# New costs for the clock that places the side chains of a hybrid decoder layer: non-urgent operations counted a third longer, and each change of engine charged

## The chip, the cores and the metric

The kernel runs on one core of one Trainium2 chip. The metric is the device time of one execution, in microseconds (us); lower is better. The same program is run several times and the median counts.

## The reference

One decoder layer over 512 tokens of width 2048, in float32:

```python
h = rms_norm(x, attn_norm_g)
proj = h @ w_in
ya = diff_attention(...)          # 4 heads, ALiBi, causal
yb = sliding_window_attention(...)  # 8 query heads, window 128, sinks
yc = rwkv7_time_mix(token_shift(rw, mu), ...)   # 16 heads of 64
x = x + concat(ya, yb, yc) @ w_out
h = rms_norm(x, ffn_norm_g)
gate, up = split(h @ w_gate_up)
x = x + (silu(gate) * up) @ w_down
return rms_norm(x, final_norm_g)
```

The RWKV part is a recurrence over time, `S = S * w + (S a) b + v k`, read out by `r`. The kernel does it in chunks of 64 steps, which needs the inverse of a triangular matrix per chunk.

## The kernel before, in words

Every large product is a stream of matrix multiplications over 128x512 tiles. A weight is split into a rounded half and a rest, as is the input, and three products of the halves are added. So one 128-column projection is 16 x 3 = 48 matmuls (`dense`, `dense_k`, L214 to L222). `sequence` (L347) runs a list of such items: one projection of the shared lora inputs, 24 for the eight RWKV pairs of heads (k, r and v of each pair), 12 for the four heads of differential attention, 6 for the sliding window, then two times 16 for the output projection (`wout_items`, L1031, 24 matmuls each) and the feed-forward part.

Everything else is cut into short steps, written as Python generators that stand in eight lanes: `rates` (decay and learning rate of a pair), `prep` (keys, transposes `bt`, products `gr`, `vt`, `bon`), `inverse` and `join` (the triangular inverse), `chain` (the recurrence over eight chunks: `z`, `u`, `S`, `y`), `post` (its normalisation `var` and gate `g`), the attention heads (`sa`, `wt`, `oa`, `sb`, `wtb`, `ob`) and `mixes`, which brings the mixers' outputs in for the output projection. After each matmul of a projection `pump` (L162) runs, while the kernel is being written, and asks of each lane whether its next step is due. It measures this with a clock of its own. `now` adds up the matmuls written so far. `free` holds, for VectorE (DVE) and ScalarE (ACT), until when their written work will keep them. `last` follows the step that is being written: when its last operation will be done. A step that yields no time of its own comes due `slack` (0.3) after `last`. So a longer `last` puts more projection matmuls between a step and the next one of its lane.

The program is static. The scheduler beneath keeps TensorE's (PE's) instructions in the written order and moves those of the other engines by its own estimate. Each engine then works its list from the top, and waits where an operand is not there.

Four places matter below.

- `prep` (L493): after `kn` (L506) come three ACT operations and eight DVE rows that end in `bk` (L526, L531). The next step transposes `bk` on PE (`bt`, L540). Ahead of it stands `while hp >= 2 and f"loop{hp - 2}" not in self.done: yield`. The tile `ar`, written first of the DVE rows after `kk` (L518), has two buffers, and the recurrence of the pair two before reads the older one until its last `y` matmul.
- `prep`, products `gr`: two rounds of 16 matmuls into the two buffers of the PSUM pool `pm`. Six masking operations on DVE (L574) empty a round. The next round, `vt`, `bon`, and the next pair's `z` and `pa` (L470, L475) use the same two buffers.
- `inverse` (L613) takes 30 small pairs of DVE operations (`xt`, `x`, L629 and L630). Then `x` is copied transposed by ACT (L633), both are written to DRAM and read back (L636, L637, L649, L651), and `join` multiplies (`pt`, then `po`, L658 and L668).
- `need` (L180): a projection's result can't be put away until an earlier pair's step is done. If it isn't, `need` moves `now` forward and writes due steps, with no projection matmuls between them. Below this is a drain.

Of the kernel before, what the change touches and what calls it, by code (L numbers as in the profile page):

```python
# [88 lines left out]
class Kernel:  # L89
    def __init__(self, tc, ins, out, dbg=None, stop=None):  # L90
        self.tc = tc
        self.nc = tc.nc
        self.i = ins
        self.out = out
        self.dbg = dbg or {}
        self.stop = stop
        self.lanes = [[], [], [], [], [], [], [], []]
        self.order = [self.lanes[j] for j in (2, 7, 6, 5, 0, 1, 3, 4)]
        self.done = set()
        self.flags = set()  # L100
        self.now = 0.0
        self.due = {}
        self.free = {"DVE": 0.0, "Activation": 0.0}
        self.last = 0.0
        self.slack = 0.3

    def col(self, name, j=0, n=P):
# [29 lines left out]
    def charge(self, ins):  # L137
        eng = str(ins.engine).split(".")[-1]
        if eng not in self.free or not ins.outs or not hasattr(ins.outs[0], "ap"):
            return  # L140
        n = math.prod(c for _, c in list(ins.outs[0].ap)[1:])
        if eng == "DVE":
            us = 0.14 + n * (0.0019 if ins.opcode == "StreamTranspose" or "Scan" in ins.opcode else 0.00104)
        else:
            us = 0.19 + n * 0.00085
        self.free[eng] = max(self.free[eng], self.now + 0.2) + us
        self.last = max(self.free[eng], self.last + us + 0.05)

    @contextlib.contextmanager
    def urgent(self):  # L150

        free = dict(self.free)
        for eng in free:
            self.free[eng] = min(free[eng], self.last + 0.3)
        with self.tc.high_priority():
            yield
        for eng in free:
            self.free[eng] = max(self.free[eng], free[eng] + 0.3)

# [1117 lines left out]
```

## Time and profile before

| | us |
|---|---|
| median of 3 runs (2480.7 to 2483.81) | 2481.95 |
| the profiled execution | 2481.82 |
| its span, first to last instruction | 2480.0 |
| PE busy in the span | 2419.3 |
| DVE busy | 1230.6 |
| ACT busy | 824.2 |
| mean granted PE clock | 0.988 |

A row of a timeline gives start, duration, engine, line, operation, output and inputs, shape and count; in brackets stands how long the engine had been idle before and what ended that. A row of a group gives busy time and the mean in ns, then the idle time before its instructions. A row of a stretch gives its ends and length, then the busy time of PE, of PE's weight loads, of DVE, ACT and POOL (GpSimd), the granted PE clock (1.00 is full speed) and the DMA share. `xcount` of an fp32 matmul counts its passes.

### The profile page before, as it was taken

The page shows a single profiled execution, that of the slowest core. Times are in us where ns is not written, and L with a number is a line of the kernel's source. Part 1 is how long each engine was busy: PE and PEld are TensorE (multiplying, and loading weights), DVE is VectorE, ACT ScalarE, POOL GpSimd, SP SyncE. Part 2 cuts the span into 40 slices and gives each one's busy share as a digit, 9 for nine tenths or more (in the row PEclk, how much of TensorE's full clock was granted, in tenths as well). Part 3 has the DMA queues.
Part 4 walks back from the last instruction along what each step waited for, and adds up shares of the span by engine and source line. Part 5 has one row for each costly group of instructions (what it writes and reads, how often), then busy time and mean ns, then how long its engine had stood idle before and what let it go on. Part 6 is the DMA issues. An engine that isn't in the chain of part 4 may idle for free.

```text
span 2480.0 us, 30228 instructions
## 1 busy us (share of the span) xinstructions
PE 2419.3 (98%) x12072; PEld 1921.0 (77%) x12072; DVE 1230.6 (50%) x2113; ACT 824.2 (33%) x1383; POOL 93.0 (4%) x117
## 2 busy tenths in 40 slices
PE   8999999989999999999999999999999999999997
PEld 6776666667677778888888888888888888888887
DVE  7587777776454544434343434343434334343437
ACT  5454555544443433322222222222222222222224
POOL 3000000000000002100000000000000000000006
PEclk9999999999999999999999999999999999999999
DMA  5222221213222423322322223232232322322224
GB/s 175 88 80 72 69 81 49 79 60 96 84 83 79 162 94 128 99 96 95 101 94 101 95 95 101 94 99 97 94 101 94 99 97 94 101 94 99 97 94 136
DMA packets 99054, 238.43 MB, mean 96 GB/s; under 512 B 30426, under 2 KB 39266, under 8 KB 98914
## 3 DMA queue, kind: packets, MB, share of 16 engines
q1 hardware_dynamic: 94018, 229.81, 28.7%
q10 hardware_dynamic: 4896, 6.69, 0.8%
q8 instruction: 95, 1.56, 0.2%
q14 instruction: 45, 0.37, 0.0%
HBM read 224.93 MB, written 11.53 MB: 95 GB/s over the span
## 4 chain that ended last, share of the span: by engine, by line
PE 91%; DVE 6%; ACT 1%; issue 1%; DMA 1%; POOL 0%; SPq 0%; DVEq 0%; ACTq 0%; POOLq 0%
PE pg L130 19%; PE pu L130 19%; PE pd L130 19%; PE po L130 7%; PE pd_k L130 4%; PE pd_r L130 3%; PE pd_v L130 2%; PE pd_va L130 2%; PE pd_qb L130 2%; PE pd_qa L130 2%; PE pd_ka L130 1%; PE z L130 1%; PE pd_l L130 1%; PE y L130 1%; PE gr L130 1%
## 5 line engine op out<-in xcount | busy, mean ns | idle before, releaser
L130 PE MATMUL pd<-al,wh_wd 128*128 128x512 f32 (+1 forms) x768 | 285.3, 371 | 0.5 <-DVE al L1127 0.5
L130 PE MATMUL pd<-ah,wh_wd 128*128 128x512 f32 (+1 forms) x768 | 285.5, 372 | 0.4 <-DVE y L1146 0.4
L130 PE MATMUL pd<-ah,wl_wd 128*128 128x512 f32 (+1 forms) x768 | 285.2, 371 | 0.0
L130 PE MATMUL pu<-x1h,wh_wu 128*128 128x512 f32 x704 | 274.3, 390 | 0.0
L130 PE MATMUL pu<-x1h,wl_wu 128*128 128x512 f32 x704 | 273.9, 389 | 0.0
L130 PE MATMUL pu<-x1l,wh_wu 128*128 128x512 f32 x704 | 273.9, 389 | 0.0
L130 PE MATMUL pg<-x1h,wh_wg 128*128 128x512 f32 x704 | 273.9, 389 | 0.0
L130 PE MATMUL pg<-x1h,wl_wg 128*128 128x512 f32 x704 | 273.9, 389 | 0.0
L130 PE MATMUL pg<-x1l,wh_wg 128*128 128x512 f32 x704 | 273.9, 389 | 0.0
L1146 DVE TENSOR_TENSOR y<-y,pd 128x512 f32<-128x512 f32 (+1 forms) x192 | 122.7, 642 | 207.7 <-PE pd L130 207.6
L207 ACT CAST wh_wd<-raw_wd 128x1024 fp32r<-128x1024 f32 x96 | 100.9, 1052 | 356.9 <-PE pd L130 177.2
L207 ACT CAST wh_wu<-raw_wu 128x1024 fp32r<-128x1024 f32 x88 | 92.7, 1053 | 366.7 <-PE pu L130 144.5
L207 ACT CAST wh_wg<-raw_wg 128x1024 fp32r<-128x1024 f32 x88 | 92.7, 1054 | 362.8 <-PE pg L130 144.9
L208 DVE TENSOR_TENSOR wl_wg<-raw_wg,wh_wg 128x1024 fp32r<-128x1024 f32 x88 | 107.8, 1225 | 171.4 <-ACT wh_wg L207 171.4
L208 DVE TENSOR_TENSOR wl_wu<-raw_wu,wh_wu 128x1024 fp32r<-128x1024 f32 x88 | 107.8, 1225 | 133.4 <-ACT wh_wu L207 133.4
L130 PEld LDWEIGHTS pd<-al,wh_wd 128*128 128x128 f32 x768 | 144.7, 188 | 25.7 <-DVE al L1127 0.8
L130 PEld LDWEIGHTS pd<-ah,wh_wd 128*128 128x128 f32 x768 | 144.7, 188 | 25.5 <-issue 0.5
L130 PEld LDWEIGHTS pd<-ah,wl_wd 128*128 128x128 f32 x768 | 144.7, 188 | 25.0
L130 PEld LDWEIGHTS pu<-x1h,wh_wu 128*128 128x128 f32 x704 | 132.2, 188 | 27.6 <-issue 0.2
L130 PEld LDWEIGHTS pu<-x1l,wh_wu 128*128 128x128 f32 x704 | 132.2, 188 | 27.6 <-issue 0.2
L130 PEld LDWEIGHTS pg<-x1l,wh_wg 128*128 128x128 f32 x704 | 132.2, 188 | 27.4
L130 PEld LDWEIGHTS pg<-x1h,wh_wg 128*128 128x128 f32 x704 | 132.2, 188 | 27.4
(340 smaller groups left out, 4155.1 us busy)
## 6 DMA issues: line engine op xcount, KB each, us to landing
raw_wd<-in_w_down SPq DMA_DIRECT2D x96, 512.0 KB, 3.2
raw_wg<-in_w_gate SPq DMA_DIRECT2D x88, 512.0 KB, 3.7
raw_wu<-in_w_up SPq DMA_DIRECT2D x88, 512.0 KB, 3.7
raw_wo<-in_w_out SPq DMA_DIRECT2D x32, 512.0 KB, 3.3
raw_k<-in_w_in SPq DMA_DIRECT2D x16, 512.0 KB, 3.7
raw_r<-in_w_in SPq DMA_DIRECT2D x16, 512.0 KB, 3.9
raw_v<-in_w_in SPq DMA_DIRECT2D x16, 512.0 KB, 3.8
x<-in_xT SPq DMA_DIRECT2D x16, 256.0 KB, 4.6
```

Source lines behind the costliest of these rows:

```text
L130: self.tc.keep_in_program_order(self.nc.tensor.matmul(out, lhsT, rhs, start=start, stop=stop))
L207: nc.scalar.copy(out=hi[:, :kn * m], in_=s)
L208: nc.vector.tensor_tensor(out=lo[:, :kn * m], in0=s, in1=hi[:, :kn * m].bitcast(F32), op=ALU.subtract)
L1146: nc.vector.tensor_tensor(out=o, in0=o, in1=ps, op=ALU.add)
```

## The change

Two fields are added. `charge`, which is called for each DVE and ACT instruction as it is written, multiplies the operation's cost by `share` (1.3, but 1.0 within `urgent`) where it extends `last`. It adds 0.15 where the engine differs from that of the operation charged before, and nothing where it is the same; it was 0.05 for each. `free` is counted as it was. `urgent` is used around the copies and updates of the recurrence (L691, L705, L713).

```diff
+        self.share = 1.3
+        self.on = None
...
         self.free[eng] = max(self.free[eng], self.now + 0.2) + us
-        self.last = max(self.free[eng], self.last + us + 0.05)
+
+        self.last = max(self.free[eng], self.last + us * self.share + (0.0 if eng == self.on else 0.15))
+        self.on = eng
...
+        share, self.share = self.share, 1.0
         with self.tc.high_priority():
             yield
+        self.share = share
```

No instruction's work changes; steps move. Lines of the changed kernel are 2, 4 or 6 higher than before. In PE's list 40 projection matmuls stand between `kn` and the first `bt` of pair 0 before and 51 now; of pair 1, 40 before and 49 now. From pair 2 on `bt` follows the recurrence of the pair two before. PE's rows from that recurrence's last `u` to `bt` of pair 3, before (r4 is the projection running there):

```order
L130 MATMUL u1_7_2438<-zs1_7_2430,linv1_482 128x64
L130 MATMUL pd_r4_2405<-xl4_133,wh_r4_0_2189 128x512
L130 MATMUL pd_r4_2405<-xh4_132,wl_r4_0_2190 128x512
L130 MATMUL pd_r4_2405<-xh5_142,wh_r4_0_2189 128x512
L130 MATMUL pd_r4_2405<-xl5_143,wh_r4_0_2189 128x512
L130 MATMUL pd_r4_2405<-xh5_142,wl_r4_0_2190 128x512
L130 MATMUL y1_2067<-gr1_1224,uv1_1360 64x64 x2
L130 MATMUL pd_r4_2405<-xh6_152,wh_r4_0_2189 128x512
L130 MATMUL pd_r4_2405<-xl6_153,wh_r4_0_2189 128x512
L134 MATMUL bt3_0_2454<-cc_76,bk3_2344 128x128 x4
```

The same place in PE's list of the changed kernel:

```order
L132 MATMUL u1_7_2468<-zs1_7_2457,linv1_482 128x64
L132 MATMUL pd_r4_2378<-xh11_198,wh_r4_8_2192 128x512
L132 MATMUL pd_r4_2378<-xl11_199,wh_r4_8_2192 128x512
L132 MATMUL pd_r4_2378<-xh11_198,wl_r4_8_2193 128x512
L132 MATMUL pd_r4_2378<-xh12_204,wh_r4_8_2192 128x512
L132 MATMUL pd_r4_2378<-xl12_205,wh_r4_8_2192 128x512
L132 MATMUL y1_2121<-gr1_1279,uv1_1455 64x64 x2
L132 MATMUL pd_r4_2378<-xh12_204,wl_r4_8_2193 128x512
L132 MATMUL pd_r4_2378<-xl13_215,wh_r4_8_2192 128x512
L136 MATMUL bt3_0_2486<-cc_76,bk3_2337 128x128 x4
```

Both the recurrence and `bt` moved 20 matmuls later within the projection; the seven between them stayed. The counts are the same in pairs 2 to 7.

The second place is the drain after the projection `ka` of head 0, where `gr` of pair 7 is needed (`need` on r7). PE's rows there before, from the first round's last product to the next projection:

```order
L130 MATMUL gr7_0_1_4925<-ar7_4742,bk7_4744 128x128
L130 MATMUL gr7_1_0_4950<-ar7_4742,bk7_4744 128x128
L130 MATMUL gr7_1_1_4951<-ar7_4742,bk7_4744 128x128
L130 MATMUL gr7_1_0_4950<-ar7_4742,bk7_4744 128x128
L130 MATMUL gr7_1_1_4951<-ar7_4742,bk7_4744 128x128
L130 MATMUL gr7_1_0_4950<-ar7_4742,bk7_4744 128x128
L130 MATMUL gr7_1_1_4951<-ar7_4742,bk7_4744 128x128
L130 MATMUL gr7_1_0_4950<-ar7_4742,bk7_4744 128x128
L130 MATMUL gr7_1_1_4951<-ar7_4742,bk7_4744 128x128
L130 MATMUL pd_va0_4993<-xh0_96,wh_va0_0_4796 128x512
```

PE's rows there now:

```order
L132 MATMUL gr7_0_1_4949<-ar7_4735,bk7_4737 128x128
L132 MATMUL gr7_1_0_4971<-ar7_4735,bk7_4737 128x128
L132 MATMUL gr7_1_1_4972<-ar7_4735,bk7_4737 128x128
L132 MATMUL gr7_1_0_4971<-ar7_4735,bk7_4737 128x128
L132 MATMUL gr7_1_1_4972<-ar7_4735,bk7_4737 128x128
L132 MATMUL pt_4977<-xnn_4964,linv0_481 32x32 x16
L132 MATMUL gr7_1_0_4971<-ar7_4735,bk7_4737 128x128
L132 MATMUL gr7_1_1_4972<-ar7_4735,bk7_4737 128x128
L132 MATMUL gr7_1_0_4971<-ar7_4735,bk7_4737 128x128
L132 MATMUL gr7_1_1_4972<-ar7_4735,bk7_4737 128x128
L132 MATMUL pd_va0_5026<-xh0_96,wh_va0_0_4769 128x512
```

`pt` of pair 6's inverse, which stood 42 projection matmuls later, now stands in the drain, in front of half of the second round. The gate `g` of pair 5 (two matmuls) also stands in the drain now, just ahead of the first round; it stood six projection matmuls earlier.

DVE's list at that place before, from the operation that puts `ka` away:

```order
L769 SCALAR_TENSOR_TENSOR ka0_4979<-pd_ka0_4806,rstd_a_435 128x512
L629 TENSOR_TENSOR xt_4554<-x_4534 32x25x6
L208 TENSOR_TENSOR wl_va0_8_4803<-raw_va0_8_4800,wh_va0_8_4802 128x1024
L574 TENSOR_TENSOR linv1_482<-gr7_0_0_4924,cc_76 64x4x64
L574 TENSOR_TENSOR zl7_4892<-gr7_0_0_4924,cc_76 64x256
L574 TENSOR_TENSOR gr7_4893<-gr7_0_0_4924,cc_76 128x256
L574 TENSOR_TENSOR linv1_482<-gr7_0_1_4925,cc_76 64x4x64
L574 TENSOR_TENSOR zl7_4892<-gr7_0_1_4925,cc_76 64x256
L574 TENSOR_TENSOR gr7_4893<-gr7_0_1_4925,cc_76 128x256
L630 TENSOR_TENSOR x_4534<-x_4534,xt_4554 32x25x6
```

DVE's list from the same operation now:

```order
L775 SCALAR_TENSOR_TENSOR ka0_5012<-pd_ka0_4779,rstd_a_435 128x512
L744 TENSOR_TENSOR ysq5_4878<-y5_4522,ysq5_4878 128x512
L214 TENSOR_TENSOR wl_va0_8_4776<-raw_va0_8_4773,wh_va0_8_4775 128x1024
L746 SCALAR_TENSOR_TENSOR ysq5_4878<-ysq5_4878,cols_75,bv5_3932 128x512
L635 TENSOR_TENSOR xt_4515<-x_4483 32x27x4
L753 SCALAR_TENSOR_TENSOR ysq5_4878<-ysq5_4878,cols_75,g5_4930 128x512
L636 TENSOR_TENSOR x_4483<-x_4483,xt_4515 32x27x4
L580 TENSOR_TENSOR linv1_482<-gr7_0_0_4948,cc_76 64x4x64
L635 TENSOR_TENSOR xt_4515<-x_4483 32x28x3
L580 TENSOR_TENSOR zl7_4924<-gr7_0_0_4948,cc_76 64x256
L636 TENSOR_TENSOR x_4483<-x_4483,xt_4515 32x28x3
L580 TENSOR_TENSOR gr7_4925<-gr7_0_0_4948,cc_76 128x256
```

And it goes on in the same alternation until the inverse's last `x` and the second round's first mask:

```order
L635 TENSOR_TENSOR xt_4515<-x_4483 32x29x2
L580 TENSOR_TENSOR linv1_482<-gr7_0_1_4949,cc_76 64x4x64
L636 TENSOR_TENSOR x_4483<-x_4483,xt_4515 32x29x2
L580 TENSOR_TENSOR zl7_4924<-gr7_0_1_4949,cc_76 64x256
L635 TENSOR_TENSOR xt_4515<-x_4483 32x30
L580 TENSOR_TENSOR gr7_4925<-gr7_0_1_4949,cc_76 128x256
L636 TENSOR_TENSOR x_4483<-x_4483,xt_4515 32x30
L580 TENSOR_TENSOR linv1_482<-gr7_1_0_4971,cc_76 64x4x64
```

Three `ysq` operations of pair 5 and the last eight of pair 6's inverse moved into the masks' place, so the inverse ends after the sixth mask.

The third place is the end of the projection v4, where `vt` and `bon` of pair 3 are needed (pair 5 at v6 is alike). PE's rows before, then now:

```order
L130 MATMUL vt3_2645<-cc_76,v3_2186 128x128 x4
L130 MATMUL pd_v4_2539<-xl15_235,wh_v4_8_2401 128x512
L130 MATMUL pd_v4_2539<-xh15_234,wl_v4_8_2402 128x512
L130 MATMUL bon3_2668<-a3_2214,rkm3_2666 128x512
L130 MATMUL pd_k5_2685<-xh0_96,wh_k5_0_2529 128x512
L130 MATMUL pd_k5_2685<-xl0_97,wh_k5_0_2529 128x512
L130 MATMUL z4_2695<-wl_453,w2_4_2691 128x512
```

```order
L132 MATMUL gr3_1_1_2636<-ar3_2335,bk3_2337 128x128
L132 MATMUL pt_2663<-xnn_2641,linv0_481 32x32 x16
L132 MATMUL vt3_2686<-cc_76,v3_2183 128x128 x4
L132 MATMUL po_2695<-linv0_481,pts_2680 32x32 x16
L132 MATMUL bon3_2728<-a3_2167,rkm3_2726 128x512
L132 MATMUL pd_k5_2747<-xh0_96,wh_k5_0_2521 128x512
L132 MATMUL z2_0_2752<-uv2_2099,zl2_1926 64x64 x2
L132 MATMUL z4_2766<-wl_453,w2_4_2762 128x512
```

The second round of `gr`, `pt`, `vt`, `po` and `bon` now stand there without projection matmuls between them. In pairs 4 and 6 it is the other way: before, `gr` (both rounds), `pt`, `po`, `vt`, `bon` and the first two chunks of a recurrence stand in a drain; now the first round and 5 projection matmuls come ahead of it, and one chunk is left in it.

## The prediction

> **What bounds the kernel now.** I read the page first: PE is busy nearly throughout.
>
> ```profile
> span 2480.0 us, 30228 instructions
> PE 2419.3 (98%) x12072; PEld 1921.0 (77%) x12072; DVE 1230.6 (50%) x2113; ACT 824.2 (33%) x1383; POOL 93.0 (4%) x117
> ```
>
> Then the stretches: mixers (60 to 826 us), first output projections, feed-forward part, tail.
>
> ```profile
> 60.00:826.00 766.00, 728.80 (x4400) 525.85 (x4399) 505.37 (x1205) 366.49 (x794) 3.04 (x30) 0.97 0.26 80
> 826.00:1021.00 195.00, 195.00 (x924) 154.97 (x923) 96.14 (x186) 74.75 (x136) 24.94 (x14) 1.00 0.34 115
> 1021.00:2410.00 1389.00, 1389.00 (x6127) 1150.15 (x6127) 538.27 (x594) 320.59 (x350) 1.78 (x1) 1.00 0.29 97
> ```
>
> PE has no idle time from 826 to 2410 us, and the moved steps end before 1021 us. So only the mixers can change: 37.2 us of PE idle time (766.00 - 728.80), and a clock of 0.97. PE's groups there say for what it waits, behind the last bar:
>
> ```profile
> L130 PE MATMUL gr<-ar,bk 64*128 64x128 f32 x256 | 24.6, 305 | 5.7 <-DVE gr L574 5.7
> L134 PE MATMUL bt<-cc,bk 128*128 128x128 f32 x64 | 12.4, 327 | 19.6 <-DVE bk L531 19.6
> L130 PE MATMUL z<-wl,w 97*128 97x512 f32 x16 | 9.5, 675 | 1.8 <-ACT uv L599 0.9 <-DMA linv<-xi 0.9
> L134 PE MATMUL wt<-cc,pa 128*128 128x128 f32 x40 | 7.2, 278 | 7.4 <-DVE pa L868 6.2 <-DVE st L861 1.2
> ```
>
> More than half is `bt` waiting for `bk`. The clock, in the last but two column, comes with such waits and with drains:
>
> ```profile
> 90.73:94.14 3.41, 1.43 (x9) 0.93 (x9) 3.33 (x5) 0.26 (x1) 0.00 (x0) 1.00 0.39 118
> 94.15:97.55 3.40, 3.40 (x13) 2.71 (x12) 0.14 (x1) 0.59 (x1) 0.00 (x0) 0.50 0.11 41
> 145.35:148.75 3.40, 3.40 (x13) 2.83 (x11) 3.33 (x8) 1.27 (x3) 0.10 (x1) 0.50 0.30 108
> ...
> 361.40:364.80 3.40, 3.40 (x18) 2.56 (x17) 1.12 (x3) 2.80 (x5) 0.10 (x1) 1.00 0.29 58
> ...
> 370.63:384.28 13.65, 12.51 (x65) 9.25 (x65) 4.80 (x13) 5.06 (x17) 0.00 (x0) 0.50 0.13 33
> ```
>
> A stretch of 3.4 us with 2 us idle is followed by one at half clock, which loses 1.7 us of work. A wait as long need not be:
>
> ```profile
> 361.19 0.65 PE L134 MATMUL bt<-cc,bk 128*128 128x128 f32 x4 [2.28 <-DVE bk L531]
> ```
>
> It is followed by full clock (the stretch from 361.40). The quoted stretches lie on a grid of 3.41 us, on which this wait falls into two of them, 1.5 and 0.8 us. The drain of pair 4 costs four stretches (the last row of the group).
>
> **The change part by part.** All instructions stay; the terms are waits and clock. A projection matmul costs 10.88 / 48 = 0.227 us:
>
> ```profile
> 1054.76 10.88 PE pu L130 x48
> ```
>
> *Pairs 0 and 1, `bt`.*
>
> ```profile
> 93.62 0.33 PE L134 MATMUL bt<-cc,bk 128*128 128x128 f32 x1 [1.99 <-DVE bk L531]
> ```
>
> ```profile
> 144.91 0.44 PE L134 MATMUL bt<-cc,bk 128*128 128x128 f32 x2 [2.52 <-DVE bk L531]
> ```
>
> Between `kn` and `bt` stand 11 and 9 more matmuls: 2.5 and 2.04 us of cover. Pair 0 gains all 1.99, pair 1 2.04. Both half-clock stretches (94.15, 145.35) should go: 2 x 1.7. Sum -7.4. Bounds: -7.9 if pair 1's wait goes whole; -4.0 if the clock falls anyway. I take -7.4, since what remains of pair 1's wait, 0.5 us, is far under the 1.5 us in one stretch that left pair 4's clock alone.
>
> At this place the Trainium skill ("TensorE: Matmul & The Clock Gate", section "Why this matters for your kernels") asks for no idle gaps of over about 3 us between bursts of matmuls, as it takes an idle window of that length to bring the half clock back; by it the term would be -4.0. The trace does not agree: a wait of 1.99 us was enough at 94.15.
>
> *Pairs 2 to 7, `bt`.* Here the added delay doesn't reach the cause.
>
> ```profile
> 276.41 0.33 PE L130 MATMUL y<-ar,uv 64*64 64x64 f32 x4
> ...
> 276.79 0.69 DVE L518 SCALAR_TENSOR_TENSOR ar<-kk,W 128x512 f32<-128x512 f32 x1 [0.42 <-PE y L130]
> ...
> 280.97 1.37 DVE L531 TENSOR_TENSOR bk<-a,IW 64x512 f32<-64x512 f32 x2
> ...
> 282.40 1.11 PE L134 MATMUL bt<-cc,bk 128*128 128x128 f32 x4 [2.22 <-DVE bk L531]
> ```
>
> DVE stands at `ar` until the last `y` of the pair two before has read the old buffer; `bk` ends 5.55 us later (282.34 - 276.79), and `bt` stands in PE's list a fixed distance behind that recurrence, seven matmuls after `u`, before and after. Between `ar` and the last `bk` DVE has the same operations and two or three of the inverse's, before and after. Term 0. Bounds -15.1 (19.6 - 1.99 - 2.52, if they all went) and +1.2 (one weight operation between, as now in pair 2).
>
> *Pair 7's drain.* Before, in order:
>
> ```profile
> 552.33 0.69 DVE L769 SCALAR_TENSOR_TENSOR ka<-pd_ka,rstd_a 128x512 f32<-128x512 f32 x1
> 552.94 0.29 DVE L629 TENSOR_TENSOR xt<-x 32x150 f32<-32x150 f32 x1
> 553.18 1.23 DVE L208 TENSOR_TENSOR wl_va<-raw_va,wh_va 128x1024 fp32r<-128x1024 f32 x1
> 554.33 0.41 DVE L574 TENSOR_TENSOR linv<-gr,cc 64x256 f32<-64x256 f32 x1
> ...
> 556.98 1.13 PE L130 MATMUL gr<-ar,bk 64*128 64x128 f32 x14 [0.76 <-DVE gr L574]
> ...
> 558.04 0.54 PE L130 MATMUL pd_va<-xh,wh_va 128*128 128x512 f32 x1
> 558.31 0.23 DVE L629 TENSOR_TENSOR xt<-x 32x84 f32<-32x84 f32 x1
> ```
>
> From `ka` (552.33) the second round is free at 4.65 us, and projections go on at 5.7. Now three `ysq` (0.73 each, the row below) and eight inverse operations (0.23 each) precede the sixth mask, less one `xt` (0.29): 4.65 + 2.2 + 1.8 - 0.3 = 8.3 us. Then comes `pt`, which needs the inverse that ended with these operations. Its way, from the previous pair:
>
> ```profile
> 551.08 0.73 DVE L747 SCALAR_TENSOR_TENSOR ysq<-ysq,cols,g 128x512 f32<-128x512 f32 x1
> ```
>
> ```profile
> 488.17 0.19 DVE L630 TENSOR_TENSOR x<-x,xt 32x30 f32<-32x30 f32 x1
> ...
> 488.92 1.95 ACT L633 COPY xtt<-x 32x1024 f32<-32x1024 f32 x1
> ...
> 490.89 0.33 SPq L637 DMA_DIRECT2D xj<-xtt  x1
> ...
> 493.75 0.44 SPq L651 DMA_DIRECT2D xnn<-xj  x1
> ...
> 495.23 1.88 PE L130 MATMUL g<-sgl,g 128*128 128x512 f32 x4
> ```
>
> The groups of loads, with the median time to landing, and `pt` over all eight pairs:
>
> ```profile
> linv<-xi SPq DMA_DIRECT2D x4, 32.0 KB, 2.0
> ```
>
> ```profile
> xnn<-xj SPq DMA_DIRECT2D x16, 32.0 KB, 3.0
> ```
>
> ```profile
> L130 PE MATMUL pt<-xnn,linv 32*32 32x32 f32 x256 | 5.8, 192 | 0.0
> ```
>
> It is 5.4 us from the end of `x` (488.36) to the issue of the last `xnn`, and 2 to 3 to land; I take 2, since the loads right behind it took that: 7.4 us. So `pt` starts at about 8.3 + 7.4 = 15.7. With it (5.8 / 8 = 0.7) and half a round of `gr` (24.6 / 32 = 0.8) projections go on at 17.2, 11.5 later than before. Of this 1.9 (`g`, the row at 495.23) and 0.7 (`pt`) are work that stood elsewhere: 8.9 us of new idle time. Behind the waiting `pt` stand half of the second round, so its masks, and the projection va0. Idle time loses nothing to the clock, but the restart should run one half stretch more than the one of before, some of it idle: +0.9. Term +9.8. Bounds: +5 (three `ysq` hidden, and the inverse ended 2 us early) and +12 (the landing at 3 us, two more stretches).
>
> *Pairs 3 and 5.* New drains of half a round, `pt`, `vt`, `po`, `bon`. Their inverses end before the first round's masks, so the DMAs have time. The masks cost PE about what they cost in the drains of pairs 4, 6 and 7 (5.7 us, 1.9 each), less 0.9 that the `z` behind these two places waits now (1.8 in two): +1.0 each, and +0.2 for the chance of a half stretch. Term +2.4. Bounds 0 and +4 each: the second is the longest `gr` wait, pair 7's (5.7 less what pairs 4 and 6 have, 3.1), and half a stretch.
>
> *Pairs 4 and 6.* Shorter drains. Pair 4's now costs 13.65 us at half clock, 1.14 of it idle: (13.65 - 1.14) / 2 = 6.3 us. I reckon that two of four stretches go (-3.4), and that `po` and `u`, no longer covered by `gr`, wait about as long as `gr` does in such a drain (+1.9). Term -1.5 each, -3.0. Bounds -4 and +2 each.
>
> *Attention.* `wt` waits 7.4 us. The wait is set by the scores two steps before: in heads 0 and 3 the same number of matmuls stands between as before; head 1 has 12 for 18 ahead of its last `wt` and head 2 ten as before. What goes at one `wt` comes at the next: 0, bounds -2 and +2.
>
> *Moved queues.* POOL's list changes by one clearing. On SP (DMA issue) the last mixer output's load now stands behind one weight load more, and its step ends 8 matmuls (1.8 us) ahead of the second half of the output projection, 68 before. First used there 18 matmuls on, it is covered by 26 x 0.227 = 5.9 us. Cost 0; without the cover, one store and load.
>
> Sum: -7.4 + 0 + 9.8 + 2.4 - 3.0 = +1.8. On the profiled execution's 2481.82 us (span 2480.0 and 1.8 around it) that is 2483.6; the median of the runs shown lies 0.13 above it, which I neglect.
>
> **The rivals.**
>
> *Slower: pairs 3 and 5 wait for their inverse too.* Place: `pt` in the drains at v4 and v6. It decides if `x` ends less than 7.4 us before PE gets to `pt`. Between the first round's end and `pt` lie 10 projection matmuls (2.3 us) and the second round (1.5); in DVE's list the last `x` stands one weight operation (1.23) and one `ysq` (0.73) ahead of the first round's masks. If DVE comes to the masks just as the round ends, that makes 5.8 us, 1.6 short. With a half stretch (1.7) each drain costs 3.3 more: 2490.2. For it: nothing but `gr` stands before `pt`. Against: DVE must have no lead over PE there, and between 276 and 283 us it reached `ar` before PE freed it.
>
> *Faster: the longer estimate covers `bt` everywhere.* Then -15.1 more and some four half stretches (-6.8): 2461.7. Against it stands the row at 276.79 with the unchanged seven matmuls.
>
> *Faster: drains of 4 and 6 lose their low clock altogether* (-4 each, for -1.5) and pair 7 is at its low bound (+5): 2473.8. For it: little is left in those drains.
>
> *Nothing:* the moved steps cost and save the same small amounts everywhere, 2481.8. The trace speaks against it in pairs 0, 1 and 7.
>
> *A wait costs only itself,* and the two half stretches come from something else: +3.4 on my sum, 2487.0; the two quoted half stretches speak against it. It is what the page of the Trainium skill named above would make of the first term.
>
> **How the numbers follow.** A measurement of this kernel can tell about 0.2%, 5 us: faster is under 2477.0, slower over 2486.9. My forecast (chance 0.50) spreads some 5 us around 2483.6: 0.36 same, 0.12 slower, 0.02 faster. First rival 0.22: slower 0.20, same 0.02. `bt` everywhere 0.05, faster. Cheap drains 0.13: faster 0.12, same 0.01. Nothing 0.07, same. Waits alone 0.03, of which 0.02 slower. Faster 0.19, same 0.47, slower 0.34. The range: down to the cheap drains, 2474; up, 2483.6 with pair 7 at +12, pairs 3 and 5 at +4 each: 2491.4, and some of the first rival with it, 2494.
>
> **What would show it.** Right: no wait of `bt` in pair 0, under 0.8 us in pair 1, full clock behind both; six waits of 2 to 4 us in pairs 2 to 7; one idle stretch of over 5 us at `pt` about 550 us; shorter half-clock stretches in the drains at v5 and qa0; `wt` at 6 to 9 us; no PE idle time from 830 to 2410 us. Wrong: `bt` of pair 3 without a wait; `pt` of pair 6 starting at once behind `gr`; waits in the recurrence (`z`, `u`, `S`); idle time at the output projection's second half.

## The result, and the profile after

The changed kernel takes 2499.81 us (median of 4 runs, 2498.82 to 2500.75), the kernel before 2481.82 (4 runs, 2480.7 to 2483.81): a ratio of 1.0075, with a 95% interval of 1.0063 to 1.0088. It is 18 us slower, where 1.8 were forecast, and outside the forecast range. The profiled execution of after took 2499.96 us, its span is 2498.2.

The first two lines of the page of after:

```profile
span 2498.2 us, 30226 instructions
PE 2432.7 (97%) x12072; PEld 1927.3 (77%) x12072; DVE 1230.7 (49%) x2113; ACT 824.5 (33%) x1383; POOL 93.8 (4%) x117
```

The engines' counts of instructions are the same, and PE is busy for 13.4 us more. The same work took longer, so the clock must have been lower somewhere. The stretches of after that answer to those of before (the mixers end 18 us later, at 844):

```profile
60.00:844.00 784.00, 740.38 (x4390) 530.98 (x4389) 503.86 (x1201) 366.32 (x793) 3.07 (x30) 0.95 0.26 79
844.00:1039.00 195.00, 195.00 (x929) 154.56 (x928) 95.46 (x187) 74.10 (x137) 24.96 (x14) 1.00 0.34 113
1039.00:2428.00 1389.00, 1389.00 (x6128) 1149.76 (x6127) 538.11 (x594) 320.49 (x350) 1.78 (x1) 1.00 0.30 97
```

All 18 us lie in the mixers; the two stretches behind them are as long as before and without idle time. PE's idle time there is 43.6 us (784.00 - 740.38), 6.4 more than before. The clock fell from 0.97 to 0.95. PE's groups show which waits came and went:

```profile
L136 PE MATMUL bt<-cc,bk 128*128 128x128 f32 x64 | 11.9, 318 | 15.7 <-DVE bk L537 15.7
L132 PE MATMUL vt<-cc,v 128*128 128x128 f32 x64 | 11.5, 337 | 3.2 <-DVE gr L580 3.2
L136 PE MATMUL wt<-cc,pa 128*128 128x128 f32 x40 | 7.5, 288 | 8.2 <-DVE pa L874 7.0 <-DVE st L867 1.2
L132 PE MATMUL pt<-xnn,linv 32*32 32x32 f32 x256 | 6.7, 198 | 6.8 <-DMA xnn<-xj 6.8
```

`bt` waits 3.9 us less, `vt` 3.2 more, `pt` 6.8 more (`vt` and `pt` waited 0.0 before). The idle time came mostly where it was forecast, but there is less of it: the terms of the prediction hold 10.7 us more on balance (-4.0 at `bt`, +8.9 in pair 7's drain, +2.0 in pairs 3 and 5, +3.8 in 4 and 6), and the mixers show 6.4. Now the stretches at half clock in the second half of the recurrent pairs (all with 0.50 in the column of the clock):

```profile
299.95:303.36 3.41, 3.41 (x40) 2.30 (x38) 0.45 (x2) 2.19 (x6) 0.00 (x0) 0.50 0.52 131
344.32:347.73 3.41, 3.34 (x10) 2.87 (x11) 3.38 (x7) 0.63 (x2) 0.10 (x1) 0.50 0.30 89
364.80:381.87 17.07, 16.30 (x80) 9.96 (x80) 6.74 (x18) 8.86 (x24) 0.10 (x1) 0.50 0.24 61
412.59:416.00 3.41, 3.26 (x9) 2.46 (x10) 3.31 (x9) 0.59 (x1) 0.10 (x1) 0.50 0.00 0
436.48:446.72 10.24, 10.24 (x55) 5.88 (x54) 2.04 (x4) 5.01 (x13) 0.10 (x1) 0.50 0.31 82
484.27:487.68 3.41, 3.41 (x12) 2.73 (x11) 3.41 (x7) 0.59 (x1) 0.10 (x1) 0.50 0.36 109
504.75:518.40 13.65, 13.23 (x72) 7.87 (x73) 4.63 (x10) 6.57 (x17) 0.00 (x0) 0.50 0.27 68
552.53:555.95 3.42, 3.42 (x9) 2.19 (x9) 3.32 (x9) 0.59 (x1) 0.00 (x0) 0.50 0.00 0
562.77:579.84 17.07, 9.91 (x90) 7.57 (x91) 4.99 (x16) 3.37 (x5) 0.00 (x0) 0.50 0.29 67
```

With 211.20 and 692.48, 3.4 us each, the mixers of after run 81.9 us at half clock; of before it was 44.4. Beside the drain of pair 4 (13.65 us, from 370.63) the last two drains of before were these:

```profile
503.75:513.99 10.24, 9.86 (x49) 7.08 (x50) 4.30 (x12) 4.81 (x15) 0.00 (x0) 0.50 0.12 27
558.36:561.77 3.41, 3.41 (x9) 2.63 (x8) 3.22 (x12) 0.00 (x0) 0.00 (x0) 0.50 0.18 31
```

What such a stretch loses is half of its busy time. Summed over all of them that is 20.8 us before and 36.4 after: 15.6 us. Idle time (6.4) and clock (15.6) make 22.0. The changed kernel also comes to its first `k` projection 1.1 us earlier (57.30 for 58.41), and 2.8 us of busy time went that neither the waits nor the clock explain; that leaves the 18.1 of the profiled pair.

The same sum can be made for all 13 traced executions of this study. The span, less the idle time of the mixers, less what their half-clock stretches lose and less added work, is 2417.5 to 2422.6 us in each of them, while the spans go from 2459.6 to 2498.7. So idle time and clock account for the differences between these kernels to within about 5 us.

### The profile page after: what moved, and what is told of

It is laid out like the page before. It is cut to its first block, busy times and chain, and to the rows that moved or that the text cites. A ratio compares the mean times of both kernels' runs of the same rounds, so it can differ in the third digit from the quotient of the medians.

```text
span 2498.2 us, 30226 instructions
## 1 busy us (share of the span) xinstructions
PE 2432.7 (97%) x12072; PEld 1927.3 (77%) x12072; DVE 1230.7 (49%) x2113; ACT 824.5 (33%) x1383; POOL 93.8 (4%) x117
## 4 chain that ended last, share of the span: by engine, by line
PE 91%; DVE 4%; ACT 2%; issue 1%; DMA 1%; POOL 0%; SPq 0%; DVEq 0%; ACTq 0%; POOLq 0%
PE pg L132 19%; PE pu L132 19%; PE pd L132 18%; PE po L132 7%; PE pd_k L132 3%; PE pd_v L132 3%; PE pd_r L132 3%; PE pd_va L132 2%; PE pd_qb L132 2%; PE pd_qa L132 2%; PE pd_ka L132 2%; PE pd_l L132 1%; PE z L132 1%; PE y L132 1%; PE S L132 1%
## 5 line engine op out<-in xcount | busy, mean ns | idle before, releaser
L132 PEld LDWEIGHTS pu<-x1h,wl_wu 128*128 128x128 f32 x704 | 132.1, 188 | 27.5
L132 PEld LDWEIGHTS pg<-x1h,wl_wg 128*128 128x128 f32 x704 | 132.1, 188 | 27.5
```

What stands on the lines that cost most here:

```text
L132: self.tc.keep_in_program_order(self.nc.tensor.matmul(out, lhsT, rhs, start=start, stop=stop))
```

## Experiments

**Which half of the change?** Two kernels, each with one half of it:

```diff
-        self.last = max(self.free[eng], self.last + us * self.share + (0.0 if eng == self.on else 0.15))
+        self.last = max(self.free[eng], self.last + us * self.share + 0.05)                               # share_only
+        self.last = max(self.free[eng], self.last + us + (0.0 if eng == self.on else 0.15))               # hop_only
```

> Only the third (share 1.3) is kept, each operation is charged 0.05 again for its hop. The order on PE has the same long runs of small matmuls between two projections as the changed kernel, of 45, 54, 45, 54 and 34 matmuls at v4 to ka0, and no bt of pairs 0 and 1 with fewer than 50 projection matmuls ahead. If the new costs act by the third alone and the loss sits in those runs: within 3 us of the changed kernel's 2499.8 (2496.8 to 2502.8). If the delay for each hop carries the loss: 2477 or less (before, and the gain of pairs 0 and 1).

> Only the delay for each hop (0.15, none on the same engine) is kept, share is 1.0. PE's order has 40 projection matmuls ahead of bt in pairs 0 and 1 as before, runs of 71 small matmuls at v4 and v6 (76 before), none at k and r, and pair 6's pt 21 projection matmuls behind the drain after ka0. If the third carries the loss: 2478 to 2486, about the kernel before. If the hops carry it: 2495 or more. A wait at that pt of up to 3 us is possible under either.

The third alone: 2500.53 us, 1.0073 of before (1.0060 to 1.0086), as the first theory has it. The hops alone: 2501.58, 1.0079 (1.0064 to 1.0093), as the other theory has it, which the first run had excluded. Yet hop_only has neither the gain of pairs 0 and 1 nor the added drains at v4 and v6 (its two runs of 71 small matmuls stand where before has its 76, behind v5 and v7, which the expectation calls v4 and v6), and it still loses as much. In its profile `bt` waits 23.4 us in place of 19.6 and `wt` 10.8 in place of 7.4, its drains are at half clock for 10.2 and 17.1 us in place of 13.7 and 10.2, and two stretches in a row stand at `bt` of pair 7.

```profile
L136 PE MATMUL bt<-cc,bk 128*128 128x128 f32 x64 | 13.2, 344 | 23.4 <-DVE bk L537 23.4
L132 PE MATMUL pt<-xnn,linv 32*32 32x32 f32 x256 | 5.8, 192 | 1.5 <-DMA xnn<-xj 1.5
```

So the halves don't add up, and no one number in the costs carries the loss. That execution took 2494.34 us at a mean clock of 0.987, 12.5 over the profiled one of before: 9.4 more idle and 6.6 more lost to the clock, less 3.5 that neither explains; the other five took 2498.39 to 2506.64 at 0.985 to 0.981. The instructions are the same in all six: 12 us between them go with the clock.

**The first term alone.** The kernel before, old costs, with `bt` of pairs 0 and 1 held back:

```diff
-        yield
+        yield self.last - self.now + 2.5 if hp < 2 else None
```

> The kernel before with its old costs, but bt of pairs 0 and 1 held back by 2.5 us of the planner's clock: 50 projection matmuls ahead of it in place of 40; from pair 3 on the order is that of before. It is the first term of the prediction alone. If that term holds by itself, at what the changed kernel's trace shows for it (4.7 us idle, 3.4 clock, 1.8 of overlap): 2472.2; at the predicted 7.4: 2474.7. If the gain is given back further on (a recurrence that starts later waits later): 2480 or more.

2475.23 us, 0.9970 (0.9960 to 0.9981): 5.8 less than the kernel before in the same series, and 0.5 above the predicted 2474.7. In its groups, 5.9 of the 19.6 us of waits are gone (the wait in pair 2 is 1.5 shorter too), and there is no half-clock stretch between 60 and 217 us. A little is given back: 2.3 us of new waits at `gr`, `pt`, `u` and `z` between 157 and 184 us, and a half stretch at `bt` of pair 4. The group of `bt`:

```profile
L134 PE MATMUL bt<-cc,bk 128*128 128x128 f32 x64 | 11.8, 316 | 13.7 <-DVE bk L531 13.7
```

**The clock behind the drains.** To the changed kernel work is added, in two drains: eight matmuls as wide as those of a projection, in front of `vt` of pairs 3 and 5. The planner's clock doesn't count them, so nothing else moves; the next projection takes over their PSUM tile and overwrites what they compute (the lines for that are left out here).

```diff
...
+        if hp in (3, 5):
+            self.spare = self.pd.tile([P, T], F32, tag="d", name=f"spare{hp}")
+            now = self.now
+            for _ in range(8):
+                self.mm(self.spare, self.fw[0][15], self.xr[15][0])
+            self.now = now
```

> The changed kernel with work added: in the drains at v4 and v6, between pt and vt of pairs 3 and 5, eight matmuls of 128x128x512 are computed into the PSUM tile of the next projection, which then overwrites them. 16 x 0.227 = 3.6 us of work more, of which 2 x 1.58 fill the wait ahead of vt; nothing else moves. Theory of the clock (the loss behind these drains is that a stretch of 3.4 us with little work in the array is followed by half clock): the half-clock stretches there (3.4 and 10.2 us) go, 2 x 1.58 + 1.7 + 5.1 - 3.6 = 6.4 us faster than the changed kernel, 2493.4. Theory of the waits (the loss is the waiting and the small matmuls themselves; the clock comes from elsewhere): 3.6 - 3.2 = 0.4 slower, 2500.2.

2492.90 us, 1.0043 (1.0031 to 1.0055): 6.9 faster than the changed kernel, for 3.6 us more work. The theory of the clock had 6.4. First the place in the changed kernel, by stretches on the grid of 3.41 us:

```profile
296.53:299.94 3.41, 1.83 (x47) 1.63 (x44) 3.12 (x6) 0.88 (x3) 0.00 (x0) 1.00 0.23 65
...
433.07:436.47 3.40, 1.82 (x48) 1.62 (x45) 3.09 (x7) 1.02 (x3) 0.00 (x0) 1.00 0.40 125
```

and the timeline of the first of them:

```profile
295.71 1.40 PE L132 MATMUL gr<-ar,bk 64*128 64x128 f32 x16
297.04 0.69 PE L132 MATMUL pt<-xnn,linv 32*32 32x32 f32 x32
299.31 1.47 PE L132 MATMUL vt<-cc,v 128*128 128x128 f32 x8 [1.58 <-DVE gr L580]
300.71 1.06 PE L132 MATMUL po<-linv,pts 32*32 32x32 f32 x32
```

PE is busy for 1.8 of 3.4 us, with `gr` and `pt`, whose stationary tiles are a half and a sixteenth of a projection's 128*128 (64*128 and 32*32). The next stretches run at half clock, 3.41 us behind the first drain and 10.24 behind the second. With the added matmuls, the same two places:

```profile
295.66 2.11 PE L133 MATMUL spare<-xh,wh_v 128*128 128x512 f32 x8
297.61 1.06 PE L133 MATMUL vt<-cc,v 128*128 128x128 f32 x8
```

```profile
297.00:304.00 7.00, 7.00 (x63) 4.65 (x61) 3.27 (x7) 5.95 (x14) 0.10 (x1) 1.00 0.38 112
427.50:434.50 7.00, 7.00 (x90) 4.86 (x86) 4.09 (x9) 4.95 (x12) 0.00 (x0) 1.00 0.37 94
```

No idle time and full clock. The wait of `vt` and the clock behind it were a loss that eight dense matmuls at this place remove; which of the two, the filled gap or the dense work, keeps the clock up can't be told from this run, since it changes both. Nor is all of the profiled gain these two places: the loss to the clock fell by 11.4 us (36.4 to 25.0), 6.8 of it here, and the rest where PE's order is the same.

**Pair 7's drain.** The changed kernel, but the drain after ka0 writes only `prep`'s lane:

```diff
...
+            order = [self.lanes[0]] if name == "r7" else self.order
-            if not self.pump():
-                self.now = min(self.due[lane[0][0]] for lane in self.order if lane)
+            if not self.pump(order):
+                self.now = min(self.due[lane[0][0]] for lane in order if lane)
```

> The changed kernel, but in the drain after ka0 (need on r7) only the lane of prep is written; the gate of pair 5, the last steps of pair 6's inverse and its pt stand behind the drain, pt 72 projection matmuls later. Between matmuls 1380 and 1640 of the projections the changed kernel takes 16.8 us more than before, 8.0 of them idle, 5.0 clock. If that is pair 6's inverse in the drain: idle time at pt gone, the half-clock stretch 3 to 7 us long in place of 17, and 2483 to 2489. If the wait only moves to where pt now stands: 2494 to 2498.

2491.91 us, 1.0042 (1.0030 to 1.0054), between the two expectations. (The 16.8 us in them hold 3.8 us of matmuls that had moved into that part.) The wait of `pt` is gone (6.8 to 0.1 over all pairs) and the half clock there is one stretch. But pair 7's recurrence starts 45 projection matmuls later than in the changed kernel, and vb must wait for it: a new drain with 6.8 us of half clock and waits in the recurrence itself. Stretches of both drains, and the rows of the new one:

```profile
557.01:560.43 3.42, 3.42 (x18) 2.91 (x19) 3.14 (x10) 0.00 (x0) 0.00 (x0) 0.50 0.15 34
662.83:669.65 6.82, 5.84 (x15) 3.04 (x16) 2.88 (x6) 3.23 (x8) 0.00 (x0) 0.50 0.59 192
```

```profile
660.71 0.50 PE L132 MATMUL S<-uv,bkn 128*64 128x64 f32 x3 [0.84 <-ACT uv L714]
...
662.17 0.65 PE L132 MATMUL z<-uv,zl 128*64 128x64 f32 x4 [0.78 <-DVE uv L725]
```

**Why `bt` waits in pairs 2 to 7, and what it hides.** DVE's rows of `prep` in another order: `kk` times `a` goes to the tile `rn`, which has done its work by then, `bk` is made from it, and `ar`, which must wait for the last `y` of the pair two before, is written after `bk`. Tried on both kernels, and on before together with the edit of bt_two:

```diff
-        ar = rp.tile([P, NCH, 2, C], F32, tag="ar", name=f"ar{hp}", bufs=2)
-        nc.vector.scalar_tensor_tensor(out=ar[:, :, 0, :], in0=c3(kk), scalar=-1.0, in1=W[:, :, 0:64], ...)
...
-        nc.vector.tensor_tensor(out=kk, in0=kk, in1=a, op=ALU.mult)
+        nc.vector.tensor_tensor(out=rn, in0=kk, in1=a, op=ALU.mult)
...
+        ar = rp.tile([P, NCH, 2, C], F32, tag="ar", name=f"ar{hp}", bufs=2)
+        nc.vector.scalar_tensor_tensor(out=ar[:, :, 0, :], in0=c3(kk), scalar=-1.0, in1=W[:, :, 0:64], ...)
         yield
```

> The kernel before, with DVE's rows of prep written in another order: kk times a goes to the tile rn, bk is made from it, and ar, which must wait for the last y of the pair two before, is written after the four bk. PE's order is the same to the matmul. If bt of pairs 2 to 7 waits because bk stands behind ar (the theory of the prediction): its six waits go, 15.1 us, and the three half-clock stretches behind them (223.85, 281.88, 490.09), 4.4: 2462.5. If bt is only the first to notice a chain that is late anyway: the waits come back at gr, vt or z, 2475 to 2482.

> The changed kernel with the same new order of DVE's rows. Its trace has six waits of bt in pairs 2 to 7, 15.7 us, and a half-clock stretch at five of them, 8.2 us of lost work. If these go: 2499.8 - 23.9 = 2476, and the drains (45, 54, 45, 54 and 34 small matmuls) cost what they cost, so that it stays 13 or more above the kernel before with the same edit. If the waits come back: 2490 to 2500.

> Both edits on the kernel before. If each wait is local and the two do not meet: 2481.9 - 9.7 - 19.4 = 2452.8. If the chain of pairs takes part of it back: 2465 or more.

On the kernel before: 2486.38 us, 1.0019 (1.0010 to 1.0028), slower, and over what either theory had. On the changed kernel: 2480.25, 0.9993 of before (0.9984 to 1.0002), 19.6 faster than the changed kernel and between its two expectations: 15.7 us of waits went at `bt`, and 7.5 came back at `pt`. With the edit of bt_two: 2483.08, 1.0009 (1.0000 to 1.0018), as the second theory has it, no sum of two gains. The groups of `bt` and `pt`, first of the kernel before with this edit (without it `bt` waited 19.6, `pt` 0.0), then of the changed kernel with it (15.7 and 6.8 without):

```profile
L134 PE MATMUL bt<-cc,bk 128*128 128x128 f32 x64 | 10.4, 287 | 3.6 <-DVE bk L528 3.6
L130 PE MATMUL pt<-xnn,linv 32*32 32x32 f32 x256 | 7.1, 204 | 17.7 <-DMA xnn<-xj 17.7
```

```profile
L136 PE MATMUL bt<-cc,bk 128*128 128x128 f32 x64 | 9.6, 272 | 0.0
L132 PE MATMUL pt<-xnn,linv 32*32 32x32 f32 x256 | 8.0, 204 | 14.3 <-DMA xnn<-xj 14.3
```

The prediction's cause of the waits is shown: with `bk` ahead of `ar` all six are gone, in both kernels. But in the kernel before they come back whole at `pt`, 8.2 us in one piece in the drain of pair 4 (behind v5) and 7.9 in that of pair 6 (behind v7):

```profile
357.29 0.19 DVE L630 TENSOR_TENSOR x<-x,xt 32x30 f32<-32x30 f32 x1
357.52 1.92 ACT L633 COPY xtt<-x 32x1024 f32<-32x1024 f32 x1 [3.06 <-DVE x L630]
...
363.73 0.31 PE L130 MATMUL pt<-xnn,linv 32*32 32x32 f32 x2 [8.21 <-DMA xnn<-xj]
```

While PE stood at `bt`, the inverse of another pair had gone on. The wait was its cover: 6.4 us pass from its last operation (357.29) to `pt`, and PE is now there too early. In the changed kernel the order itself has most of that cover: no wait of `pt` in these two drains is over 1.5 us, and the edit gains. The longest one there, 6.5 us, is in pair 7's drain. So the sign of the change turns with this edit: 2486.38 without the change, 2480.25 with it, where 13 us to the other side were expected.

**Putting it together.** The changed kernel with both edits (`bk` first, only `prep` in pair 7's drain), and the same with added matmuls in two drains (v4, v6) and in four (at pairs 3 to 6):

> The changed kernel with ar written after the four bk, and with only prep's lane written in the drain after ka0. The first edit alone gave 2480.25 and the second alone took 7.9 from the changed kernel. If the idle time at pt in that drain (7.2 us) and its 20 us of half clock go and come back only in part, as in the second edit alone: 2470 to 2475. If the recurrence of pair 7, which starts 72 projection matmuls later, takes it all back at kb: 2478 to 2482.

> The kernel above, with eight matmuls of 128x128x512 more between pt and vt in the drains at v4 and v6 (into the next projection's PSUM tile, overwritten by it): 3.6 us of work more. The wait of vt that they filled is 0.9 us now, or is taken up by pt. Theory of the clock: the half-clock stretches behind these two drains (3.4 and 10.2 us, 6.8 of lost work) go, 2 to 4 us faster than the kernel above. Theory of the waits: 2.5 to 3.6 slower.

> The same with eight such matmuls also ahead of vt of pairs 4 and 6, in the longer drains at k and r: another 3.6 us of work. There the half-clock stretches are 17.1 and 10.2 us (12.8 of lost work), and the run of small matmuls goes on behind the added ones (vt, z, u, bon, S, y, z, pa). Theory of the clock: at most half of it is saved, 0 to 3 us faster than the kernel with eight in two drains. Theory of the waits: 3 to 4 slower than that.

Without added work 2470.59, 0.9950 (0.9937 to 0.9964), as the first theory has it (the drain in which the recurrence takes its part back is at vb, not at kb). With eight in two drains 2470.76, 0.9959 (0.9946 to 0.9971): neither expectation; the added 3.6 us of work were paid for and no more. Here `pt` itself waits ahead of them (1.2 and 1.0 us), so the eight matmuls begin at 291.98 and 421.47, just as the stretch with the small matmuls ends, and run at half clock themselves:

```profile
288.36:291.77 3.41, 1.83 (x47) 1.53 (x47) 2.85 (x7) 0.00 (x0) 0.00 (x0) 1.00 0.42 66
291.77:295.18 3.41, 3.41 (x20) 2.67 (x15) 0.11 (x1) 0.73 (x2) 0.00 (x0) 0.50 0.26 58
```

In these runs the dense work kept the clock up where it fell into that stretch, as in filled, and not where it came behind it. With eight in four drains 2465.23, 0.9933 (0.9921 to 0.9946): 5.5 less than with two, where 0 to 3 were expected. It is the fastest kernel of this study, 16 us ahead of before, though its PE does 7.3 us of work for nothing (32 x 0.227). The last long drain, with two and with four:

```profile
486.33:503.39 17.06, 16.57 (x84) 10.15 (x86) 5.26 (x15) 8.86 (x24) 0.00 (x0) 0.50 0.16 43
```

```profile
484.00:501.00 17.00, 15.78 (x103) 10.36 (x103) 13.45 (x37) 13.33 (x32) 0.00 (x0) 1.00 0.14 40
```

In the first it runs at half clock for 17 us, in the second never. In the mixers of the second only four stretches of 3.4 us are left at half clock, and the mean clock of its profiled run is 0.995. These two executions are the slowest of their five (2475.33) and the fastest (2461.37), so they show the difference larger than it is; the mean clock of all five is 0.988 to 0.992 with two, 0.992 to 0.995 with four.

## Why the prediction was wrong

The places were seen, and most waits there were near their size. The step that failed is the clock in the drains. The terms hold 10.7 us more idle time and 8.9 us less loss to the clock (-3.4 for pairs 0 and 1, +0.4, -6.8 and +0.9 for the three kinds of drains); the mixers of the profiled pair show 6.4 more idle time and 15.6 more loss to the clock. The failed step stands in three sentences of the prediction: "I reckon that two of four stretches go (-3.4)" for pairs 4 and 6, "+0.2 for the chance of a half stretch" for 3 and 5, and "the restart should run one half stretch more" for 7. Of the terms, with what the two profiles show for them (idle time and clock):

- *Pairs 0 and 1, `bt`: -7.4.* Measured -8.1: both waits and both half stretches went. bt_two keeps most of the gain by itself (5.8). Right.
- *Pairs 2 to 7, `bt`: 0.* Measured +4.2. The waits went from 15.1 to 15.7 us, and their cause is the one named (bk_first). But five of them, in place of three, are followed by a half stretch: +3.6 of clock. Whether a wait of 2 to 3 us costs one depends on how it falls on the grid, as the prediction had seen at 361.19, and then held fixed. (The stretch from 361.40 that it quotes there isn't on that grid, which has a boundary at 360.39; the split of the wait into 1.5 and 0.8 us is right.)
- *Pairs 3 and 5, new drains: +2.4.* Measured +8.2: 1.4 idle (`vt` 3.2, less 1.8 at `z`) for the 2.0 priced, and 6.8 of clock for the 0.4 that stood there. The prediction had looked for a long wait (its bound of 4 took the longest `gr`), while a wait of 1.6 between `pt` and `vt` was enough. filled, which takes both away, shows it.
- *Pairs 4 and 6, shorter drains: -3.0.* Measured +4.3: 0.8 idle and 3.6 of clock. The drains got shorter by count, 54 small matmuls for 76, but not in time at half clock: 17.1 and 13.7 us for 13.7 and 10.2. `z` over `wl` and `pa`, fp32 products of 512 columns, had stood behind the first projection matmuls and now close the drain; in pair 4's they hold PE for 2.8 us at half clock (372.42 to 375.21) before it gets to projections again. How much of the 3.6 belongs to the order is open. In share_only, r7_prep_only and filled, which have the same order here, the two drains run 13.7, 20.5 and 23.9 us at half clock together (30.7 in the changed kernel), and in before and bt_two 23.9 and 20.5. On average the shorter drains ran as long at half clock as the longer ones: the two stretches each that the forecast took off did not go.
- *Pair 7's drain: +9.8.* Measured +9.4: 6.2 idle for the predicted 8.9, 3.3 of clock for 0.9. The size was right by luck, by two errors against each other. `pt` of pair 7 itself waits 1.5 more, which no term had.

```profile
563.79 0.77 PE L132 MATMUL gr<-ar,bk 64*128 64x128 f32 x2 [3.15 <-DVE xt L635]
565.50 1.19 PE L132 MATMUL gr<-ar,bk 64*128 64x128 f32 x6 [0.94 <-DVE x L636]
571.27 0.31 PE L132 MATMUL pt<-xnn,linv 32*32 32x32 f32 x2 [4.58 <-DMA xnn<-xj]
572.20 1.06 PE L132 MATMUL pt<-xnn,linv 32*32 32x32 f32 x30 [0.61 <-DMA xnn<-xj]
```

- *Attention: 0.* +1.7, one half stretch (692.48). `wt` waits 0.8 more, `sa` and the transposes of `va` (`p_van`) as much less. Within its bound of 2. The queues of POOL and SP: 0, as said.

These make 21.2, and small waits elsewhere bring them to the 22.0 of the first section but for rounding; less its 2.8 and 1.1 that is the measured 18. The first rival (pairs 3 and 5 wait at `pt`) did not happen; its time, 2490.2, lay nearer only by chance.

A second thing the prediction had not seen, though no term failed by it: it treated the waits as losses, each in its place. The waits also hang together in a chain from pair to pair (`bt`, `gr`, inverse, `pt`, recurrence, and `bt` two pairs on). A wait taken out at one link comes back at the next that has no cover: at `pt` in bk_first, at vb in r7_prep_only. That the two halves of the change cost 18 us each and not more together may come from this, which is not shown. Which of its waits and stretches would make hop_only slow in its median run (clock 0.983, 7 us over the profiled one) isn't settled: only that one execution has a trace.

## What to carry to other kernels

In a kernel like this one, count the projection matmuls in each stretch of the clock's grid, not the idle gaps alone: where a planner collects small matmuls between two products, price the half clock that can follow, and try some products in between, where the gap is and not behind it. Before taking out a wait, ask what else runs under it, and look at the next link of the chain for cover. A table of costs that is off by a third can change where waits fall more than how long they are, so its effect is read from the places, one by one, and a change that loses alone may gain beside another.

## What the hardware showed that was not expected

Work that computes nothing made the kernel faster: 3.6 us of it saved 6.9 us on the changed kernel. On the last kernel the first 3.6 us saved nothing, and 3.6 more in the two longer drains saved 5.5.

A stretch of 3.41 us with 1.8 us of small matmuls and no gap over 1.6 us was followed by half clock. The Trainium skill ("TensorE: Matmul & The Clock Gate", section "Why this matters for your kernels") asks for no idle gaps over about 3 us; here the trace does not agree, since far shorter ones were enough when the rest of the stretch was small matmuls. Not even those were needed: in the kernel before, this stretch has only 0.44 us idle and no projection in it, and the four stretches from 370.63 behind it are at half clock.

```profile
367.22:370.62 3.40, 2.96 (x78) 2.30 (x76) 3.22 (x8) 1.57 (x5) 0.00 (x0) 1.00 0.59 184
```

The stretch that ends at 360.39 had 1.5 us idle, the rest of it largely projections, and full clock followed. So the small matmuls count, and not the idle time alone. What exactly decides stays open: the stretch from 496.92, with 0.19 us idle and no projection either, was followed by full clock.

Half clock can last though PE is fully busy. Of two drains with the same instructions, one was followed by one such stretch (299.95) and the other by three:

```profile
436.48:439.88 3.40, 3.40 (x41) 2.58 (x39) 0.60 (x2) 2.19 (x6) 0.00 (x0) 0.50 0.71 180
439.89:443.30 3.41, 3.41 (x9) 1.21 (x8) 1.45 (x2) 0.83 (x2) 0.08 (x1) 0.50 0.03 10
443.31:446.71 3.40, 3.40 (x9) 2.08 (x8) 0.00 (x0) 1.97 (x5) 0.01 (x1) 0.50 0.19 57
```

They begin 0.15 us apart on the grid (295.71 and 432.39, which is 40 stretches of 3.413 us and 0.15). In share_only and r7_prep_only, whose order has the same two drains, the second was followed by 6.8 and 3.4 us. Executions of one kernel differ too: those of hop_only by 12 us (0.5%), at mean clocks of 0.987 to 0.981, 29 of before by 7.8 us (2479.04 to 2486.79). That it is the place on the grid that makes them differ is likely, but not shown, since each kernel has one trace.
